# A TensorE warm-up of ten float32 matmuls of 128 columns in place of twenty of 64

## The chip, the cores and the metric

The kernel is one program on one core of a Trainium2 chip. The metric is the device time of one execution in microseconds, from the chip's own clock. A core has engines that run side by side, each with its own queue of instructions: TensorE (PE in the profile, with its weight loads shown apart as PEld), VectorE (DVE), ScalarE (ACT), GpSimd (POOL) and SyncE (SP), which here issues nearly all transfers from the chip's main memory. Semaphores order them.

## The reference

It is a small decoder of two layers over 256 tokens of width 2048, in float32. Layer 0 mixes by a gated short convolution, layer 1 by multi-head latent attention with 16 heads; each is followed by a squared-ReLU MLP of width 8192, and each of the four sub-layers by a layer norm of the scaled residual. Only the start matters here, the mixer of layer 0:

```python
bcu = x @ w_in                              # (256, 2048) @ (2048, 6144)
gate_b, gate_c, u = jnp.split(bcu, 3, axis=-1)
v = gate_c * u
y = causal_depthwise_conv(v, conv_w)        # width 3
return (gate_b * y) @ w_out
```

## The kernel before

Activations are kept transposed: 128 channels on the partitions, 256 tokens along the free axis, 16 such tiles (k = 0 to 15) for the width of 2048. A product of 128 output channels is a sum over k into one PSUM bank.

Float32 operands are split for speed. ACT casts a weight tile to `hi` (line 116) and DVE puts the rest into `lo` (line 117); the activations are split the same way into a tile of 512 columns, high part and low part side by side (lines 519 and 520). For each k, `high` (line 192) multiplies the high weights by all 512 columns, and `low` (line 196) the low weights by the 256 columns of the high part.

The start of the program:

- **Warm-up.** DVE sets the tile `ones` (128x128, line 348). TensorE then runs `WARM` plain float32 matmuls of `ones` by itself into a PSUM bank `warm` that nobody reads (lines 349 to 351). They are first in TensorE's queue; all its real work stands behind them. `ones` serves again later, for means in the norms (line 396).
- **Opening.** The first four products (`HEAD = 4`) are computed together, so that TensorE can start with few data. x and the four weight columns (`first`) come in pieces of k that grow: `FIRST = (0, 1, 2, 4, 6, 8, 12, 16)`. The pieces are loaded, cast and split in this order (lines 513 to 523). `opening` (line 255) runs each piece for the four products, first the high weights, then the low ones. For k = 0 the high part is done in two halves of 256 columns (`high_early`, line 185, and `high_late`, line 188). These products are the tiles `ps_g`.
- **Streamed products.** The other 44 products of `w_in` take their weights from a stream of 512 KB halves (`raw`, loaded at line 127, split at lines 116 and 117), two halves to a product of 16 k. `lagged` (line 232) runs the `low` matmuls eight steps behind the `high` ones. These are the tiles `ps_l`.

After that come the convolution, the output product, the first MLP, attention and the second MLP, all fed by the same stream of weights. Plain float32 matmuls occur in a few places: sums for the norms with one column (`stat`, line 438), attention scores of 128 and 256 columns (`S`, lines 824 and 825) and some more.

The program's text gives the order of work, and the language's own scheduler interleaves instructions within an engine at build time: the early and late halves of k = 0 alternate in the trace, though the text has all early ones first.

Of the kernel before, what the change touches and what calls it, by code (L numbers as in the profile page):

```python
# [16 lines left out]
P = 128  # L17
# [20 lines left out]
FIRST = (0, 1, 2, 4, 6, 8, 12, 16)  # L38
HEAD = 4
GROUP = 3  # L40
WARM = 20
TURNED = 2
LAG = 8
WO_G = 3
# [6 lines left out]
def trunk(ctx: ExitStack, tc: tile.TileContext, xT, vecs, w_first, w_in, w_out, w_kv, w_q, w_uk, w_uv,  # L51
          w_qn, w_qp, w_o, w1, w2, w2f, cosT, sinT, mask, ident, gb, out):
    nc = tc.nc
# [126 lines left out]
    def psum(name):  # L180
        return Banks.next().tile([P, 512], F32, tag="mm", name=name)
# [164 lines left out]
    ones = const.tile([P, P], F32, name="ones")  # L346
    col = const.tile([P, 4], F32, name="col")
    nc.vector.memset(ones, 1.0 / P)
    warm = psum("warm")
    for _ in range(WARM):  # L350
        nc.tensor.matmul(warm[:, :P // 2], ones, ones[:, :P // 2], start=True, stop=True)
    nc.vector.memset(col[:, 0:1], 1.0 / D)
    nc.vector.memset(col[:, 1:2], 1.0 / RK)

# [708 lines left out]
```

## Time and profile before

| | |
|---|---|
| median of 3 runs | 2036.47 us (2036.33 to 2037.58) |
| the profiled execution, its own time | 2036.62 us |
| its span, first to last instruction | 2034.8 us |
| PE busy | 2028.2 us, 11260 matmul records |
| PEld (weight loads) busy | 1767.8 us |
| DVE, ACT busy | 1636.9 us, 1186.6 us |
| read from main memory | 381.25 MB, 188 GB/s over the span |

All starts below are microseconds from the start of the span. A busy TensorE in these rows is one whose matmuls follow each other; the length of one record includes its way through the array, so that records overlap and the pace is the distance from start to start. A plain float32 matmul leaves two records, and so the twenty of the warm-up show as x40. In a timeline row, like instructions are merged: start, time to the last end, engine, line, operation, tiles and shape, count, and in brackets the idle time before it and what ended that.

### The profile page before, as it was taken

The numbers are of one execution on the slowest core, as the hardware profiler recorded it, in microseconds if no ns is written. First come the engines' busy times: TensorE is split into PE (matmuls) and PEld (weight loads), VectorE is DVE, ScalarE is ACT, GpSimd is POOL, SyncE is SP. The second block draws the span as 40 slices with busy tenths as digits, with TensorE's granted clock in tenths as the row PEclk, the third lists the DMA queues.
The fourth block names the chain that finished last, engine by engine and source line by source line (L and its number), as shares of the span: only waits on it lengthen the run. The fifth ranks groups of instructions, "written<-read, shape, count | busy, mean of one in ns | idle before, by whom it ended". The sixth has DMA issues, their size and how long they took to land.

```text
span 2034.8 us, 30232 instructions
## 1 busy us (share of the span) xinstructions
PE 2028.2 (100%) x11260; PEld 1767.8 (87%) x11260; DVE 1636.9 (80%) x2559; ACT 1186.6 (58%) x1849; POOL 4.5 (0%) x25
## 2 busy tenths in 40 slices
PE   9999999999999999999999999999999999999998
PEld 8888888988888888888889998898888888888886
DVE  7667667677898988979778978776889898898966
ACT  6444445576565565656656655567656556566561
POOL 0000000000000000000000000000000000000000
PEclk9999999999999999999999999999999999999999
DMA  8666666564747557475754543656474665746673
GB/s 286 213 188 188 192 189 188 170 204 135 256 146 228 174 189 247 143 233 162 242 184 145 176 137 128 194 168 206 135 247 146 218 203 160 251 143 225 187 230 121
DMA packets 106851, 385.32 MB, mean 189 GB/s; under 512 B 11856, under 2 KB 12752, under 8 KB 106448
## 3 DMA queue, kind: packets, MB, share of 16 engines
q1 hardware_dynamic: 105984, 381.17, 59.7%
q8 instruction: 88, 1.44, 0.3%
q0 software_dynamic: 576, 2.10, 0.3%
q14 instruction: 59, 0.48, 0.1%
q10 hardware_dynamic: 144, 0.13, 0.0%
HBM read 381.25 MB, written 2.10 MB: 188 GB/s over the span
## 4 chain that ended last, share of the span: by engine, by line
PE 99%; DVE 0%; issue 0%; DVEq 0%
PE ps_u L192 20%; PE ps_l L192 13%; PE ps_u L196 11%; PE ps_d L276 7%; PE ps_d L277 7%; PE ps_d L278 7%; PE ps_l L196 7%; PE ps_f L278 4%; PE ps_f L276 4%; PE ps_f L277 4%; PE ps_w L226 1%; PE ps_w L224 1%; PE ps_w L225 1%; PE ps_g L226 1%; PE ps_g L224 1%; PE ps_g L225 1%
## 5 line engine op out<-in xcount | busy, mean ns | idle before, releaser
L117 DVE TENSOR_TENSOR lo<-raw,hi 128x1024 fp32r<-128x1024 f32 x710 | 858.9, 1221 | 274.9 <-ACT hi L116 202.7
L116 ACT CAST hi<-raw 128x1024 fp32r<-128x1024 f32 x710 | 741.2, 1050 | 428.0 <-DMA raw<-in_w_dram 126.5
L192 PE MATMUL ps_u<-xhl,hi 128*128 128x512 f32 x1792 | 621.3, 391 | 0.0
L196 PE MATMUL ps_u<-xhl,lo 128*128 128x256 f32 x1792 | 499.6, 280 | 0.0
L192 PEld LDWEIGHTS ps_u<-xhl,hi 128*128 128x128 f32 x1792 | 334.3, 187 | 72.5
L196 PEld LDWEIGHTS ps_u<-xhl,lo 128*128 128x128 f32 x1792 | 338.6, 189 | 1.7
L276 PE MATMUL ps_d<-hi,h 128*128 128x512 f32 x640 | 249.8, 390 | 0.0
L277 PE MATMUL ps_d<-lo,h 128*128 128x512 f32 x640 | 249.3, 389 | 0.0
L278 PE MATMUL ps_d<-hi,h 128*128 128x512 f32 x640 | 249.1, 389 | 0.0
L192 PE MATMUL ps_l<-xhl_a,hi 128*128 128x512 f32 x704 | 244.1, 393 | 0.0
L196 PE MATMUL ps_l<-xhl_a,lo 128*128 128x256 f32 x704 | 195.4, 279 | 0.0
L192 PEld LDWEIGHTS ps_l<-xhl_a,hi 128*128 128x128 f32 x704 | 132.1, 188 | 29.9
L278 PEld LDWEIGHTS ps_d<-hi,h 128*128 128x128 f32 x640 | 120.1, 188 | 25.3
L276 PEld LDWEIGHTS ps_d<-hi,h 128*128 128x128 f32 x640 | 120.1, 188 | 25.1
L277 PEld LDWEIGHTS ps_d<-lo,h 128*128 128x128 f32 x640 | 120.2, 188 | 24.7
L196 PEld LDWEIGHTS ps_l<-xhl_a,lo 128*128 128x128 f32 x704 | 131.9, 188 | 0.2
L597 ACT ACTIVATE fh<-fh 128x256 f32<-128x256 f32 x112 | 46.6, 416 | 92.0 <-DVE fh L333 92.0
L192 PE MATMUL ps_l<-z,hi 128*128 128x512 f32 x240 | 82.4, 391 | 0.0
L116 ACT CAST hi_t<-raw_t 128x1024 fp32r<-128x1024 f32 x48 | 50.6, 1054 | 52.2 <-DVE raw_t L149 30.4
L226 PE MATMUL ps_w<-xd,hi 128*128 128x258 f32 x256 | 72.7, 285 | 0.0
L224 PE MATMUL ps_w<-xd,hi 128*128 128x258 f32 x256 | 72.5, 284 | 0.0
L225 PE MATMUL ps_w<-xd,lo 128*128 128x258 f32 x256 | 72.3, 282 | 0.0
(253 smaller groups left out, 3191.6 us busy)
## 6 DMA issues: line engine op xcount, KB each, us to landing
raw<-in_w_dram SPq DMA_DIRECT2D x416, 512.0 KB, 4.5
raw<-in_w2f_dram SPq DMA_DIRECT2D x96, 512.0 KB, 3.6
raw<-in_w_in_dram SPq DMA_DIRECT2D x88, 512.0 KB, 4.2
raw<-in_w_out_dram SPq DMA_DIRECT2D x32, 512.0 KB, 4.0
raw<-in_w_o_dram SPq DMA_DIRECT2D x32, 512.0 KB, 4.1
raw<-in_w_kv_dram SPq DMA_DIRECT2D x10, 512.0 KB, 3.6
raw<-in_w_q_dram SPq DMA_DIRECT2D x8, 512.0 KB, 4.2
raw<-in_w_uk_dram SPq DMA_DIRECT2D x8, 512.0 KB, 4.2
```

What stands on the lines that cost most here:

```text
L116: nc.scalar.copy(hi, src)
L117: nc.vector.tensor_tensor(lo, src, hi.bitcast(F32), ALU.subtract)
L192: nc.tensor.matmul(ps, w[blk // 8][0][:, blk % 8, :], x, start=first, stop=False)
L196: nc.tensor.matmul(ps[:, :T], w[blk // 8][1][:, blk % 8, :], x[:, :T], start=False, stop=last)
L224: nc.tensor.matmul(ps[:, :W], hi, x[k][:, :W], start=k == 0, stop=False)
L225: nc.tensor.matmul(ps[:, :W], lo, x[k][:, :W], start=False, stop=False)
L226: nc.tensor.matmul(ps[:, :W], hi, x[k][:, W:], start=False, stop=k == NC - 1)
L276: nc.tensor.matmul(ps, x[0], w[0], start=first, stop=False)
L277: nc.tensor.matmul(ps, x[0], w[1], start=False, stop=False)
L278: nc.tensor.matmul(ps, x[1], w[0], start=False, stop=last)
L597: nc.scalar.activation(f, f, AF.Relu)
```

## The change

The warm-up runs ten matmuls over all 128 columns of `ones` instead of twenty over the first 64. The columns that pass through TensorE are 1280 in both.

```diff
-WARM = 20
+WARM = 10
...
     nc.vector.memset(ones, 1.0 / P)
     warm = psum("warm")
     for _ in range(WARM):
-        nc.tensor.matmul(warm[:, :P // 2], ones, ones[:, :P // 2], start=True, stop=True)
+        nc.tensor.matmul(warm[:, :P], ones, ones, start=True, stop=True)
     nc.vector.memset(col[:, 0:1], 1.0 / D)
```

## The prediction

> **What bounds the kernel.** First the page: which engine is busy, and which one the chain that ended last runs over.
>
> ```profile
> PE 2028.2 (100%) x11260; PEld 1767.8 (87%) x11260; DVE 1636.9 (80%) x2559; ACT 1186.6 (58%) x1849; POOL 4.5 (0%) x25
> ...
> PE 99%; DVE 0%; issue 0%; DVEq 0%
> ```
>
> TensorE is the bound from end to end. The view of waits, for PE alone, says how much room it has:
>
> ```profile
> PE offset L961 <- DVE udiag L959: 1.2, 1, 1.2
> PE warm L351 <- DVE col L353: 1.1, 1, 1.1
> PE lnAB L376 <- DVE rr L371: 0.3, 1, 0.3
> ```
>
> It waits 2.6 us in all, and nowhere between the warm-up and the last norms. So a microsecond that TensorE gains or loses in the opening moves the end by a microsecond, unless another engine becomes late. All else is a question of the first 34 us, in the timeline of all engines (start, length, engine, line, tiles, count):
>
> ```profile
> 1.05 8.79 PE L351 MATMUL warm<-ones 128*128 128x64 f32 x40 [1.05 <-DVE col L353]
> 4.64 0.89 ACT L116 CAST hi<-first 128x128 fp32r<-128x128 f32 x4
> ...
> 6.46 0.89 DVE L117 TENSOR_TENSOR lo<-first,hi 128x128 fp32r<-128x128 f32 x4
> ...
> 9.12 1.32 ACT L116 CAST hi<-first 128x256 fp32r<-128x256 f32 x4 [0.59 <-DMA first<-in_w_first_dram]
> 9.54 0.55 PEld L185 LDWEIGHTS ps_g<-xhl_a,hi 128*128 128x128 f32 x2
> ...
> 11.46 1.05 PE L196 MATMUL ps_g<-xhl_a,lo 128*128 128x256 f32 x4
> ...
> 12.31 1.83 PE L192 MATMUL ps_g<-xhl_a,hi 128*128 128x512 f32 x4
> ...
> 14.46 2.00 PE L192 MATMUL ps_g<-xhl_a,hi 128*128 128x512 f32 x8
> ...
> 16.30 1.12 PE L196 MATMUL ps_g<-xhl_a,lo 128*128 128x256 f32 x8
> 17.00 2.18 ACT L116 CAST hi<-first 128x512 fp32r<-128x512 f32 x4 [1.45 <-DMA first<-in_w_first_dram]
> ...
> 17.25 2.00 PE L192 MATMUL ps_g<-xhl_a,hi 128*128 128x512 f32 x8
> ```
>
> and, in a later window, the first work after the opening:
>
> ```profile
> 34.10 1.98 PE L192 MATMUL ps_l<-xhl_a,hi 128*128 128x512 f32 x8
> ```
>
> Two things are to be seen. The weights of k=0 are cast from 4.64 on, but their matmuls (L185) begin at 9.54, when the warm-up ends: data lie ready for nearly 5 us behind it. And real work starts at half speed: four passes of 256 columns take 12.31-11.46=0.85 us (0.213 each), later eight take 17.25-16.30=0.95 (0.119). Two answers say when that ends and what the warm-up's passes look like:
>
> ```profile
> 13.60 0.58 PEld L196 LDWEIGHTS ps_g<-xhl_a,lo 128*128 128x128 f32 x2
> ```
>
> ```profile
> L351 PEld LDWEIGHTS warm<-ones x40: 288/333/333, 1.1 to 9.3; 128*128 128x128 f32 x40
> ```
>
> A weight load takes 333 ns in the warm-up and until 13.60, and 188 ns from 14.0 on. The full clock therefore comes at about 13.9, after some 4.3 us of gapless real work; 8.5 us of warm-up did not bring it. (The granted clock reads 1.00 in these windows, so durations show this, not that column.)
>
> **What the change does, and its price.** A float32 matmul is two passes in the records: 40 passes of 64 columns become 20 of 128. Nothing else changes: no wait, tile, DMA or queue. The one memset ahead is the same, and ACT, DVE and SP wait for nothing of TensorE before 27 us.
>
> *Length of the warm-up.* Now (9.54-1.05)/40=0.212 us a pass. The new pass does not occur at half speed. From below: it costs what one of 64 columns does, if the weight load sets the pace; from above, twice that, 0.424, if the columns do. The nearest rows are float32 passes at full speed:
>
> ```profile
> 385.41 0.50 PE L438 MATMUL stat<-col,S 128*128 128x1 f32 x4
> 385.77 0.58 PE L438 MATMUL stat<-col,Q 128*128 128x1 f32 x4
> 386.22 0.36 PE L224 MATMUL ps_w<-xd,hi 128*128 128x258 f32 x1
> ```
>
> ```profile
> 1140.99 0.38 PE L824 MATMUL S<-kqva 128*128 128x128 f32 x2
> 1141.21 0.39 PE L825 MATMUL S<-kpe,kqva 128*128 128x128 f32 x2
> ```
>
> Passes of one column come every (386.22-385.41)/8=0.10 us, passes of 128 columns every 0.22/2=0.11. So up to 128 columns a pass costs its weight load, and I take 0.212: 20 passes, 4.25 us, and the first real load comes at 9.54-4.25=5.3 instead of 9.54.
>
> [...]
>
> *When the full clock comes.* If what opens it is columns streaming without gaps, which real work showed for 4.3 us, the new warm-up streams all of its time where the old one did about half (64 columns in a slot that holds 128). Counted from 1.05 that is 5.4. A start at 5.3 leaves no gap: casts of k=0 are done by 5.53, its low parts by 6.0.
>
> *The sum.* At full speed k=0 is 12 passes of 0.119 (1.43 us), k=1 four of 0.23 and four of 0.119 (1.40). From 5.3 that ends at about 8.2; their last low part is there at 7.35 (6.46+0.89). Then TensorE waits for k=2 and 3: the cast begins at 9.12, its first quarter ends near 9.5, so the passes start at about 9.6. They are the passes that started at 14.46, and from there to 34.10 they took 19.64 us, all at full speed. New end of the opening: 9.6+19.64=29.24, a gain of **4.86 us**. Later data: k=8 to 11 are needed at 9.6+8.4=18.0 and first cast by 17.6; k=12 to 15 at 23.6, cast by 21.5; the first streamed weights at 29.2, cast by 24.9. Afterwards one chunk of work takes 16x0.35=5.6 us and two halves of weights, which land 1.26 us apart at this stage (casts at 23.86, 25.12, 26.38): the weights keep up. ACT's wait of 5.45 us for the first result, until 32.87, shrinks and hides the rest of the shift.
>
> Cover is thin at one place only, 18.0 against 17.6. TensorE now idles about 1.4 us before 9.6, which costs nothing more: the DMA sets that time.
>
> The profiled execution took 2036.62 us (span 2034.8 plus 1.8), 0.15 over the median of 2036.47. 2036.62-4.9 gives **2031.7 us**.
>
> **Rivals.**
>
> *The warm-up still opens nothing* (its operand is constant, its passes float32; the old one did not open it in 8.5 us). Then the real work starts at half speed, 4.25 us earlier, and reaches full speed 4.3 us later as before. All moves by 4.25: k=2 starts at 10.2, its data are there, 2032.4. It could come later still: each microsecond more at half speed costs 0.455 (from 0.119/0.213 and 0.23/0.427). If the spread of the three runs before (1.25 us) is the opening's, it wanders by 1.25/0.455=2.7 us, up to some 6.4 after the start of real work, and the case reaches 2033.4.
> [...]
>
> *Same length*: passes of 0.424 us. Real work starts at 9.54 again, but after a warm-up that streams all the time, at full speed: 1.43+1.40+19.64=22.5 us from 9.6, so 32.1 in place of 34.1 and 2034.6. Half way between the bounds, 0.32, real work starts at 7.4 and the end is 29.9: 2032.4.
>
> *Slower*: the clock falls back while TensorE waits for data before 9.6, and the passes of k=2 on run at half speed again. Each microsecond so costs 0.455. It takes until 9.6+4.86/0.455=20.3 to eat the gain, until 29 to lose 4 us more. For it: the idle 1.4 us are new, and so is running close behind the casts. Against it: at half speed TensorE falls behind the data and so runs without gaps, which opened the clock in 4.3 us before; one such relapse costs 2.0 us and leaves 2033.7.
>
> **The numbers.** The main case 0.67 (2031.7), the warm-up that opens nothing 0.14, longer passes 0.09, a relapse that leaves part of the gain 0.06, slower 0.04. A measurement of this kernel tells about 0.2%, 4.1 us, from no change: under 2032.4 is faster. The main case and a third of the second lie there, less a little for the small distance of 0.7 us: 0.70 faster, 0.26 same, 0.04 slower. The range: below, the earliest that the data allow (casts of k=8 at 17.6 plus 11.3, so 28.9 and 2031.4), less the runs' own spread, 2030.7; above, the same-length case, 2034.6.
>
> **What would show it.** Twenty records of L351 that end near 5.3, the first L185 there; weight loads of 188 ns by about 8; idle PE before 9.6, put down to ACT or DMA; the first ps_l at L192 near 29.2; nothing new in PE's waits after that. Wrong if L351 ends past 7, if loads of 333 ns go on beyond 10, or if PE waits for hi or lo after 30 us.

## The result, and the profile after

The changed kernel takes 2032.08 us (median of 14 runs, 2031.62 to 2035.56), the kernel before 2036.55 (14 runs): a ratio of 0.998, 95% interval 0.9972 to 0.9988. The prediction was 2031.7 us. The profiled execution took 2031.86 us, its span is 2030.0. Of all runs below, two fell far out at a much lower granted clock, one without a warm-up (2861.94 us at 0.655) and one of the kernel before (2493.78 at 0.753), and nothing here rests on them.

The page says the same as before, less 5.4 us of PE (20 records of the warm-up and a faster start):

```profile
PE 2022.8 (100%) x11240; PEld 1763.4 (87%) x11240; DVE 1637.1 (81%) x2559; ACT 1186.2 (58%) x1849; POOL 4.5 (0%) x25
...
PE 99%; DMA 0%; DVE 0%; issue 0%; SPq 0%; ACT 0%; DVEq 0%
```

The view of waits, PE alone, has one new row, the third:

```profile
PE offset L961 <- DVE udiag L959: 1.2, 1, 1.2
PE warm L351 <- DVE col L353: 1.1, 1, 1.1
PE ps_g L192 <- ACT hi L116: 0.6, 1, 0.6
PE lnAB L376 <- DVE rr L371: 0.3, 1, 0.3
```

The timeline of the opening shows where that is:

```profile
1.05 4.34 PEld L351 LDWEIGHTS warm<-ones 128*128 128x128 f32 x20 [1.05 <-DVE col L353]
...
5.27 0.55 PEld L185 LDWEIGHTS ps_g<-xhl_a,hi 128*128 128x128 f32 x2
...
8.37 0.63 PE L196 MATMUL ps_g<-xhl_a,lo 128*128 128x256 f32 x4
...
9.13 1.33 ACT L116 CAST hi<-first 128x256 fp32r<-128x256 f32 x4 [0.62 <-DMA first<-in_w_first_dram]
...
9.58 2.08 PE L192 MATMUL ps_g<-xhl_a,hi 128*128 128x512 f32 x8 [0.58 <-ACT hi L116]
...
16.80 2.18 ACT L116 CAST hi<-first 128x512 fp32r<-128x512 f32 x4 [1.44 <-DMA first<-in_w_first_dram]
...
18.04 3.88 PE L192 MATMUL ps_g<-xhl_a,hi 128*128 128x512 f32 x16
```

and, in a later window:

```profile
29.30 1.98 PE L192 MATMUL ps_l<-xhl_a,hi 128*128 128x512 f32 x8
```

The warm-up's loads end and real work starts at 5.27 (before: 9.54). k=0 and k=1 are done by about 8.85, TensorE waits for the cast of k=2, goes on at 9.58 (these passes started at 14.46 in the kernel before) and reaches the first streamed product at 29.30 instead of 34.10. From there to the end of the span it is 2000.7 us in both (2034.8-34.10 and 2030.0-29.30). The whole change lies in the opening: 4.80 us. The two traces have the same instructions in the same order on every engine, apart from the warm-up.

The weight loads show the clock:

```profile
6.34 0.33 PEld L185 LDWEIGHTS ps_g<-xhl_a,hi 128*128 128x128 f32 x1
6.56 0.37 PEld L188 LDWEIGHTS ps_g<-xhl_a,hi 128*128 128x128 f32 x2
```

Loads take 333 ns until 6.5 and about 190 from then on. The trace also keeps a record of the clock's state, which begins when the full clock first opens (the mean granted clock counts the time ahead of it as full speed, and so reads 1.00 there). It opens at 6.7, 5.6 us after the warm-up began; in the trace of the kernel before it opened at 13.9.

### The profile page after: what moved, and what is told of

It is laid out like the page before. It is cut to its first block, busy times and chain, and to the rows that moved or that the text cites. A ratio compares the mean times of both kernels' runs of the same rounds, so it can differ in the third digit from the quotient of the medians.

```text
span 2030.0 us, 30192 instructions
## 1 busy us (share of the span) xinstructions
PE 2022.8 (100%) x11240; PEld 1763.4 (87%) x11240; DVE 1637.1 (81%) x2559; ACT 1186.2 (58%) x1849; POOL 4.5 (0%) x25
## 4 chain that ended last, share of the span: by engine, by line
PE 99%; DMA 0%; DVE 0%; issue 0%; SPq 0%; ACT 0%; DVEq 0%
PE ps_u L192 20%; PE ps_l L192 13%; PE ps_u L196 11%; PE ps_d L276 7%; PE ps_d L277 7%; PE ps_d L278 7%; PE ps_l L196 7%; PE ps_f L278 4%; PE ps_f L276 4%; PE ps_f L277 4%; PE ps_w L226 1%; PE ps_w L224 1%; PE ps_w L225 1%; PE ps_g L226 1%; PE ps_g L224 1%; PE ps_g L225 1%
## 5 line engine op out<-in xcount | busy, mean ns | idle before, releaser
L192 PE MATMUL ps_u<-xhl,hi 128*128 128x512 f32 x1792 | 621.3, 391 | 0.0
L192 PEld LDWEIGHTS ps_u<-xhl,hi 128*128 128x128 f32 x1792 | 334.4, 187 | 71.9
L192 PE MATMUL ps_l<-xhl_a,hi 128*128 128x512 f32 x704 | 244.1, 393 | 0.0
L192 PEld LDWEIGHTS ps_l<-xhl_a,hi 128*128 128x128 f32 x704 | 132.2, 188 | 29.8
L192 PE MATMUL ps_l<-z,hi 128*128 128x512 f32 x240 | 82.4, 391 | 0.0
```

The costliest lines, as they stand in the source:

```text
L192: nc.tensor.matmul(ps, w[blk // 8][0][:, blk % 8, :], x, start=first, stop=False)
```

## Experiments

Two theories. **Columns**: a pass costs its weight load up to 128 columns, the full clock opens only on gapless columns, and after the change the arrival of k=2 sets the opening's end. **Rivals**: any activity, or only real work, opens the clock; or the warm-up's work on the clock is what the gain comes from. The edits are shown against the changed kernel. For each run the useful reading is when real work starts, when the clock opens, and when the first streamed product starts (29.30 after, 34.10 before).

**Fewer matmuls, as sparse as before.**

```diff
-        nc.tensor.matmul(warm[:, :P], ones, ones, start=True, stop=True)
+        nc.tensor.matmul(warm[:, :P // 2], ones, ones[:, :P // 2], start=True, stop=True)
```

> Ten float32 matmuls of 64 columns: the length alone, with the columns as sparse as before. A pass of 64 columns costs its weight load, so the warm-up ends near 5.3 as after the change (both theories). Theory 1, only gapless columns open the full clock: loads of 333 ns go on into real work until 9.0 to 11.7, k=2 starts near 10.2 instead of 9.58, and the time is 2032.4 to 2033.4, some 0.4 to 1.4 us over the changed kernel. Rival, any activity opens it about 5.6 us after its start: loads of 188 ns from 6.7, k=2 at 9.58, 2032.0.

Measured: 2032.37 us (11 runs, 2031.74 to 2033.42). The weight loads of this run:

```profile
9.33 1.11 PEld L196 LDWEIGHTS ps_g<-xhl_a,lo 128*128 128x128 f32 x4
10.37 0.77 PEld L192 LDWEIGHTS ps_g<-xhl_a,hi 128*128 128x128 f32 x4
```

and its first streamed product:

```profile
30.11 1.98 PE L192 MATMUL ps_l<-xhl_a,hi 128*128 128x512 f32 x8
```

Four loads still spread over 1.11 us from 9.33; from 10.4 they keep the pace of the full clock. The clock opened at 10.3, 5.0 us after real work began at 5.3, and the first streamed product came at 30.11. Ten sparse matmuls, 4.2 us of them, opened nothing, as the theory of columns (theory 1 in the expectations) had it. Against before, the shorter warm-up alone moves the opening by 34.10-30.11=3.99 us; the denser columns add 30.11-29.30=0.81.

**As many matmuls, dense.**

```diff
-WARM = 10
+WARM = 20
```

> Twenty float32 matmuls of 128 columns: the dense columns alone, as many matmuls as before. Theory 1: the warm-up by itself opens the clock, at about 6.7 (5 to 7.9), while no real work has run; the passes after that come every 0.11 us, so the warm-up ends near 8.2 instead of 9.5; real work runs at full speed from its first load, k=2 starts near 11.1, the first streamed product near 30.8, and the time is 2033.5 (2033.0 to 2034.6). Rival, only real work opens the clock: 40 passes of 0.213 us to 9.57, loads of 333 ns until 13 to 15, 2036.5 as before.

Measured: 2033.08 us (11 runs, 2032.30 to 2033.68). The warm-up's rows by tile, and the first real loads:

```profile
L351 PEld LDWEIGHTS warm<-ones x40: 192/333/338, 1.1 to 8.2; 128*128 128x128 f32 x40
```
```profile
8.27 0.54 PEld L185 LDWEIGHTS ps_g<-xhl_a,hi 128*128 128x128 f32 x4
```

A shortest load of 192 ns in the warm-up itself: the clock opened at 6.9, before any real work. It then ended early, at 8.27, and real work ran at full speed from its first pass; the first streamed product came at 30.86 (expected 30.8). So dense columns opened the clock here, 5.9 us after their start and without real data, and the 1.56 us against the changed kernel are TensorE's queue behind a longer warm-up.

**No warm-up**: lines 349 to 351 taken out.

> No warm-up at all. Theory 1 with the sum of the prediction: real work starts when its first casts are done, near 5.0, at half speed, without gaps; the clock opens 4.3 to 6.4 us later, at 9.3 to 11.4; k=2 starts at 9.8 to 10.2; the time is 2032.0 to 2033.0, within 1 us of the changed kernel, because the data of k=2 arrive at 9.5 in any case. Rival, the warm-up is worth what it was put there for: the clock opens only at 13 or later and the time is 2034 or more.

Measured: 2032.12 us (11 runs), first streamed product at 29.76.

```profile
PE ps_g L185 <- ACT hi L116: 5.1, 1, 5.1
```
```profile
29.76 1.98 PE L192 MATMUL ps_l<-xhl_a,hi 128*128 128x512 f32 x8
```

TensorE waits 5.1 us for its first cast, starts at half speed (three loads of L192 still take 1.18 us from 7.86; at full speed the kernel before has eight in 1.70 from 14.34), and the clock opens at 9.8. Of the 4.80 us gained, 34.10-29.76=4.34 are had by taking the warm-up away altogether; what the new one does for the clock is worth the other 0.46 here. (Here, as in the runs of twenty by 128 and of twenty by one, the scheduler also puts the early and late halves of k=0 in the text's order.)

**The changed kernel again**, beside these three.

> The changed kernel once more, unchanged, beside the others: 2032.0 in most runs, spread under 1 us, since k=2 waits for its cast at 9.5 whatever the clock does before 8. In a run whose clock stands at 0.999 instead of 1.0 the time is longer by 2 us or more (a relapse to half speed after the idle stretch before k=2: 0.455 us for each microsecond). Rival: long runs have the same clock as the short ones.

Measured: 2031.82 us (10 runs, 2031.25 to 2032.14), all at a clock of 1.0; 29.25 in its profile. No long run came up, so it says nothing on their cause. Beside it, by the medians, the kernel with ten sparse matmuls is 0.55 us longer and the one without a warm-up 0.30, where the single profiles put it at 0.81 and 0.46.

**One column.**

```diff
-WARM = 10
+WARM = 20
...
-        nc.tensor.matmul(warm[:, :P], ones, ones, start=True, stop=True)
+        nc.tensor.matmul(warm[:, :1], ones, ones[:, :1], start=True, stop=True)
```

> Twenty float32 matmuls of one column. If the weight load sets the pace up to 128 columns, 40 passes of 0.213 us: the warm-up ends near 9.55 as before the change, the clock opens 4.3 to 6.4 us after real work begins, and the time is that of before, 2036 to 2037. Rival, columns set the pace: the warm-up is over by 3 us and the time is that of no warm-up, 2032.1.

Measured: 2036.72 us in one run, the time of before.

```profile
L351 PEld LDWEIGHTS warm<-ones x40: 288/333/338, 1.1 to 9.3; 128*128 128x128 f32 x40
L351 PE MATMUL warm<-ones x40: 352/352/373, 1.1 to 9.4; 128*128 128x1 f32 x40
```

Forty passes of one column take as long (last start 9.4) as forty of 64. With the dense runs this settles the price that the prediction had between 0.212 and 0.424: 0.213 us a pass at half speed, for 1, 64 and 128 columns. So the columns did not set the pace of these passes; that the weight load does is the likely reading, and no run shows it by itself.

**Longer idle time before k=2.** The next two make the piece after k=1 larger, so that its data come later.

```diff
-FIRST = (0, 1, 2, 4, 6, 8, 12, 16)
+FIRST = (0, 1, 2, 6, 8, 12, 16)
```

> The changed kernel with k=2 to 5 in one piece, FIRST = (0, 1, 2, 6, 8, 12, 16): TensorE idles from 8.85 until the cast near 11.7, some 2.8 us. Theory, arrival of data sets the opening's end: first streamed product near 31.4, 2033.9. Theory on the two long runs of the changed kernel (2034.02 and 2035.56 at a clock of 0.999), that an idle stretch here lets the clock fall back to half speed: loads of 333 ns return after 11.7 in some or all runs, those have a clock of 0.999 or less and 2 us or more on top, 2036. Rival, idle time of this length does nothing to the clock: all runs at 1.0 and 2033.9.

Measured: 2035.57 us (11 runs). Three runs at a clock of 1.0 took 2033.62 to 2034.19, as was expected from the arrival of data alone (2033.9); eight at 0.999 or 0.998 took 2035.53 to 2037.56. The profile, of a run of 2037.18, has the long wait and, by windows (PEclk is the number after POOL's), the clock at half:

```profile
PE ps_g L192 <- ACT hi L116: 3.6, 1, 3.6
```
```profile
6.00:12.00 6.00, 2.68 (x19) 2.30 (x17) 2.51 (x7) 2.04 (x5) 0.00 (x0) 1.00 0.99 380
12.80:16.00 3.20, 3.20 (x9) 2.46 (x8) 3.20 (x8) 3.20 (x8) 0.00 (x0) 0.50 1.02 428
16.50:20.00 3.50, 3.50 (x24) 3.21 (x23) 3.36 (x6) 2.70 (x5) 0.00 (x0) 1.00 1.00 403
```

The idle stretch ran from about 8.5 to 12.26; the clock closed at 12.74, half a microsecond after work had resumed, and opened again at 16.15: 3.41 us at half speed, about 1.6 us lost. The rest of its excess lies elsewhere (last section).

```diff
-FIRST = (0, 1, 2, 4, 6, 8, 12, 16)
+FIRST = (0, 1, 2, 8, 12, 16)
```

> The changed kernel with k=2 to 7 in one piece, FIRST = (0, 1, 2, 8, 12, 16): TensorE idles from 8.85 until near 13.7, some 4.8 us. Without a relapse the first streamed product comes near 33.4, 2035.9. With the relapse that the long runs suggest, loads of 333 ns return and the clock opens again only 4.3 to 6.4 us after 13.7, and the time is about 2 to 3 us longer, 2038 to 2039.

Measured: 2038.96 us (10 runs, 2038.17 to 2039.66), every run at 0.999 or 0.998. TensorE idled some 6 us, from 8.2 to 14.18; the clock was at half from 11.70 to 18.53, and the first streamed product came at 35.88. Idle time closed the clock here: by their granted clock of 0.999 or 0.998, in eight of eleven runs with some 3.6 us of it, and in all ten with some 6.

**Smaller pieces.** If the arrival of k=2 binds, giving it a piece of its own should help.

```diff
-FIRST = (0, 1, 2, 4, 6, 8, 12, 16)
+FIRST = (0, 1, 2, 3, 4, 6, 8, 10, 12, 16)
```

> The changed kernel with the opening's data in smaller pieces, FIRST = (0, 1, 2, 3, 4, 6, 8, 10, 12, 16). Theory: after the change the bound of the opening is the arrival of k=2 and 3, for which TensorE idles from 8.85 to 9.58. With k=2 alone in a piece its cast is done near 8.9, the idle time goes, and the first streamed product moves from 29.30 to 28.4 to 28.7: 2031.0 to 2031.3, and no run with a clock under 1.0. Rival, the transfers or the casts of the extra pieces cost as much as they save (ten more casts on ACT and on DVE, four more transfers): 2031.8 or more.

Measured: 2031.36 us (7 runs), a ratio to before of 0.9972 (0.9961 to 0.9983). The passes of k=1 and k=2 now join:

```profile
8.49 0.64 PE L196 MATMUL ps_g<-xhl_a,lo 128*128 128x256 f32 x4
8.96 1.09 PE L192 MATMUL ps_g<-xhl_a,hi 128*128 128x512 f32 x4
```

The wait before k=2 is gone and the first streamed product starts at 28.75 (expected 28.4 to 28.7, so the gain is a little smaller than expected). To compare it with the changed kernel itself, both ran again on one chip:

> The changed kernel on the chip of the next three, for a comparison among them: 2031.8 to 2032.1, and a run now and then at a clock of 0.999 and 2 us longer.

> The changed kernel with smaller pieces, FIRST = (0, 1, 2, 3, 4, 6, 8, 10, 12, 16), beside it: 0.4 to 0.6 us under it (first streamed product at 28.75 instead of 29.3), 2031.2 to 2031.6, all runs at a clock of 1.0. Rival, the difference seen before was one between chips: the same time.

Measured: 2032.00 us (11 runs, 2031.67 to 2033.72) for the changed kernel, 2031.26 (10 runs, 2030.70 to 2032.89) for the smaller pieces; eight of the latter's ten lie below the lowest of the former. Expected were 0.4 to 0.6 us; the opening's end differs by 29.21-28.82=0.39 in the two profiles. This version is the fastest here: 0.9975 of before (0.9966 to 0.9984). Two runs of each were 1.1 to 1.7 us long at a clock of 1.0, which the expectation did not have. In this second profile the clock opened earlier, at 5.4, and TensorE again waits for data, now for k=4:

```profile
PE ps_g L192 <- ACT hi L116: 0.3, 1, 0.3
```

So in this trace data bind the opening once more.

Last, the two factors apart, smaller pieces without a warm-up and with the old one:

> The smaller pieces without any warm-up. Theory: nothing of the opening waits for data now, so the half-speed stretch counts in full: real work from 5.1, clock open near 9.8, 0.455 x 4.7 = 2.1 us lost, first streamed product at 5.1+22.5+2.1=29.7, 2032.3; the warm-up of ten by 128 is worth about 0.9 us here. Rival, the warm-up is worth as little as with the larger pieces: within 0.3 us of the kernel beside it.

> The old warm-up (twenty by 64) with the smaller pieces. Theory: there the length of the warm-up sets the start, and no data are late, so smaller pieces bring nothing: 2036.6 as before. Rival, smaller pieces help by themselves: 2036.1.

Measured: 2032.03 us without a warm-up, first streamed product at 29.81 (expected 29.7), by the medians 0.77 us over the kernel with both; and 2036.73 with the old warm-up, 34.13, a ratio to before of 1.0001 (0.9992 to 1.001). Smaller pieces bring nothing while the old warm-up holds TensorE, and once they have removed the wait, the clock that the new warm-up opens is worth 29.81-28.82=0.99 us instead of 0.46 by the profiles, 0.77 instead of 0.30 by the medians:

```profile
29.81 2.01 PE L192 MATMUL ps_l<-xhl_a,hi 128*128 128x512 f32 x8
```
```profile
28.82 2.01 PE L192 MATMUL ps_l<-xhl_a,hi 128*128 128x512 f32 x8
```

## Why the prediction was right

- **Length.** Passes of 0.212 and a start at 5.3: 5.27 measured, and the runs of one and of 128 columns show the same 0.213 us a pass. The rival of longer passes is out.
- **The clock.** Dense columns opened it, sparse ones did not: shown by the two runs that change one of the two (twenty of 128 at 6.9, within the warm-up; ten of 64 not in 4.2 us, only real work at 10.3). Nor did 8.5 us of passes of one column or of 64, so that the rival of any activity is out here. The size was off. The prediction had one case, 4.3 us, and took 5.4 for the opening; it came at 6.7. Over the profiled runs with dense warm-ups it came 3.4 to 5.9 us after the start. This moved nothing, because k=0 and k=1 still ended before the cast of k=2. That the room sufficed was in part luck: in the second run of the changed kernel the clock opened at 7.0, and its view of waits has only 0.4 us before k=2.
- **The bound by data.** 9.6 predicted, 9.58 measured; 29.24 against 29.30. The idle time before it, counted from pass to pass as in the prediction, was 9.58-8.85=0.7 us, not 1.4 (the view of waits has 0.6, since it counts to the end of the last record): the late clock took the rest, 0.455x(6.67-5.27)=0.6. The thin place at 18.0 held (cast from 16.80, passes at 18.04).
- **Nothing later absorbs it.** 2000.7 us from the first streamed product to the end in both.
- **The rival of a relapse** was not idle talk. The step shown in the profile of the longer idle stretch, half speed for 3.4 us, costs 1.6; two of the 14 runs of the changed kernel, 2034.02 and 2035.56, had a clock of 0.999 and are long by 2.0 and 3.5. That these were relapses after the short wait is inferred from clock and time, and stays unshown: neither left a trace, none came up in 21 later runs, one such step does not make up 3.5, and one of 32 runs of the kernel before, which has no such wait, stood at 0.999 as well (2037.54). No run of the changed kernel reached the slower side; in the profile of the longer idle stretch the clock opened again after 3.41 us at half speed, in which TensorE was busy throughout (3.20 of the 3.20 us from 12.80), as the prediction had argued.
- **The sign.** The medians differ by 4.47 us (0.22%), the profiles by 4.8: just over the bound of 0.2%, as the small distance of 0.7 us in the prediction implied. The interval, 0.12 to 0.28%, takes in the bound, so on which side of it the result fell is in part luck.

## What to carry to other kernels

A warm-up stands in TensorE's queue ahead of real work: let it end when the first data arrive, and look at what waits behind it before looking at the clock. Measure the kernel without it too: taking the old one away gave 4.34 of the 4.80 us here. Fill its passes with as many columns as cost no more time, since passes of 64 columns here took as long as those of 128 (0.213 us at half speed) and opened nothing. Then find the next bound: once the warm-up was short, smaller first pieces of data, which brought nothing with the old one, became worth 0.4 to 0.7 us.

## What the runs showed of the hardware that was not expected

- The clock's state changed at distances of 3.41 us or a multiple of it: by the record it was open for 6.83 us and at half for 3.41 (12.74 to 16.15) in the trace with some 3.6 us of idle time, open for 6.83 and at half for 6.83 (11.70 to 18.53) in the one with some 6, and the long open state lasted 2020.69 us in the kernel before and 2024.10 in the changed one, 3.41 apart. In the first of these traces it closed 0.48 us after work had resumed (12.74 against 12.26). An estimate from these numbers: if steps of 3.41 us run on back from each opening (no record shows them there), they would also account for its scatter. At the nine openings given above, dense passes (of 128 columns, or real work) then fill the last step from end to end, and of the step before that between 0.48 and 2.53 us, or 74% (the opening at 7.0, less 3.41, less the start at 1.05). By this estimate a step filled to 74% did not open the clock.
- The warm-up's own passes came nearly twice as fast once the clock had opened (in the run of twenty by 128 every 0.213 us up to 6.9, and from there, by the 7.30 us that its loads take in all, about 0.11), so that real work began at 8.27 after twenty dense matmuls, 1.3 us before the 9.54 after twenty sparse ones.
- From the first streamed product to the end, eleven of the fourteen profiles have 2000.6 to 2000.9 us, and three (both of the longer idle stretches and the old warm-up with smaller pieces) some 1.1 to 1.3 us more. In the one with some 6 us of idle time it is lost between 1250 and 1330 us, at the attention's output product: its passes of 512 columns take 72.2 us from the first to the last start where the kernels before and after take 70.9, and the median record of the 208 is 398 ns long against 391. The one with the old warm-up lost as much at a mean granted clock of 1.0, which fits the few long runs at that clock. The cause stays open.
